# Two expert layers: 240 instead of 256 tokens meet every expert, the others gather their experts' rows

## The chip, the cores and the metric

One core of a Trainium2 chip runs the whole program. The metric is the device time of one execution in microseconds (us). The kernel before took 2565.35 us (median of three runs, 2559.76 to 2567.32). The engines are TensorE (PE; its weight loads are listed apart as PEld), VectorE (DVE), ScalarE (ACT), GpSimd (POOL) and SyncE (SP, which here only queues DMA transfers).

## What is computed

One inference step of a two-layer decoder trunk for 304 tokens: 16 meta tokens, 256 prompt tokens and 32 sample tokens (8 sequences of 4). Layer 0 mixes tokens by gated linear attention and an RG-LRU, layer 1 by RWKV-7. After each mixer comes a PEER expert layer, which is what the change touches. D is 1024, and there are 128 x 128 = 16384 experts of one neuron each:

```python
def block(xb):                                   # tokens x 1024
    q = (xb @ w_q).reshape(..., 8, 256)          # 8 heads, normalised
    s1 = einsum('thd,hkd->thk', q[..., :128], keys[:, 0])
    s2 = einsum('thd,hkd->thk', q[..., 128:], keys[:, 1])
    # top 16 of each, top 16 of their 256 sums: 16 experts a head
    gate = softmax(sc)
    act = gelu(einsum('thkd,td->thk', u_tab[eidx], xb))
    return einsum('thk,thkd->td', gate * act, v_tab[eidx])
```

So each token uses 8 x 16 = 128 rows of `u_tab` and as many of `v_tab`. The layer's result is LN(alpha * x + peer(x)). All is float32. The 16 meta tokens' outputs are dropped at the end, so layer 1 computes its expert layer for 288 tokens only.

## The kernel before

The program runs mixer 0, expert layer 0, mixer 1 and expert layer 1 one after the other. `peer(xh, xl, l)` (L747) is an expert layer. The activations lie transposed (128 features x 304 tokens, 8 blocks `k`), as a pair `xh` + `xl` of float32r tiles whose sum is the float32 value; the rows of the profile print such tiles as f32. A product in this split form (`mm3`, L174) is three matmuls for each block: wh*xh, wh*xl, wl*xh.

Two ways of meeting the experts stand side by side. **Dense tokens** (`d0` to `g0`, L752: 256 of them) meet all 16384 experts in 128 steps `e` of 128 experts. `up` (L991) multiplies 128 experts' rows of u with the dense tokens into `ps_u`; ScalarE applies gelu (L1001) and leaves `act`. `weigh` (L1016) multiplies `act` on VectorE by a dense table of gates (zero where a token didn't choose the expert) and splits it. `down` (L1033) multiplies it with 128 rows of v: two tiles of 128 tokens (stationary), two halves of 512 features, three terms, 12 matmuls into `ps_mm`, summed over 124 steps. The last four steps go through `into` (L1049). For the first 24 steps `up` is a plain float32 matmul, which the program issues as two instructions a block; for the other 104 it is the split form. The weights of a step are loaded whole (`raw`, 512 KB), rounded by ScalarE (`wh`, L170), and the rest is taken by VectorE (`wl`, L171).

**Gathered tokens** (`g0` to the end: `ng` is 48 in layer 0, 32 in layer 1) fetch only their own rows. They come in groups of 16 or 32 tokens (`groups`, L756). In a group of n tokens the 128 partitions hold 128/n of each token's 128 row numbers, in n columns. For each column an indirect DMA, issued by GpSimd (`rows`, L1089), brings 128 rows of 4 KB, two columns to a buffer, three buffers (`ab`). `gup` (L1096) multiplies such a column by the token's activations and sums (one VectorE instruction of 128x1024 and an accumulator read), `gdown` (L1107) adds the row times its coefficient to a sum. Before it, `gprep` (L1058) spreads the row numbers, gates and activations over the partitions with the 0/1 matrix `k_rep`; after it, `gsum` (L1117) folds the partitions back with small matmuls against `k_diag`. Layer 0 has 16 + 32 columns for each table, layer 1 has 32: 160 gathers in all.

The dense gate table is made before the main loop: `ggroup` (L951), once for each 8 tokens (32 times a layer), builds one-hot matrices on VectorE (four products, L959 to L962), multiplies them on TensorE (16 matmuls of 128 columns, `ps_s<-ab`) and ScalarE moves them out (L970); every second one is stored to `G` in DRAM. `gates_load` (L1011) reads 8 steps' gates back, 1 MB at a time (`gb<-G`).

The order is planned by due times (`at`, L769, and L1134 to L1195) in units of about a microsecond of the main loop: the queries, the top-16 search, `ggroup` every `gs` = 2.85 units, then from `tw` on one `up` and one `down` every 2 x 2.56 units, with `up` 36 steps ahead. Gathers are spread evenly from 15 units behind `tw` to 40 before the end (`tg` units apart for two columns: 10.6 in layer 0, 15.9 in layer 1), first all of u, then all of v; the multiplies follow `lag` = 20 units behind their gather. The framework's scheduler may still move an instruction ahead of others on its engine when its inputs are there.

Of the kernel before, what the change touches and what calls it, by code (L numbers as in the profile page):

```python
# [32 lines left out]
GN_EPS = 64e-5  # L33
CHUNKS = [(16 * c, 16) for c in range(17)] + [(TP + 4 * s, 4) for s in range(8)]
TT = [(0, 128), (128, 128), (256, 48)]
XW = 3 + TP + 8 * 7
# [3 lines left out]
def _consts():  # L40
# [20 lines left out]
    for s in range(8):  # L61
# [3 lines left out]
    p, r = np.arange(P)[None], np.arange(P)[:, None]  # L65
    c["k_rep"] = np.stack([r == 16 + p % 32, (r == p % 16), (r == p % 32), r // 32 == p // 32, r // 16 == p // 16],
                          axis=1).astype(np.float32)
# [114 lines left out]
class Prog:  # L182
# [564 lines left out]
    def peer(self, xh, xl, l):  # L747
# [3 lines left out]
        d0 = 0 if l == 0 else NM  # L751
        g0 = d0 + 256  # L752
        ng = T - g0
        tiles = [(d0, P), (d0 + P, P), (g0, ng)]
        groups = ([(0, 16)] if ng == 48 else []) + [(ng - 32, 32)]
        with ExitStack() as es:  # L756
# [6 lines left out]
            gb = lambda shape, dt=F32: self.t(pr, shape, dt, "gb", 4)  # L763
            G = self.t(dp, [16, P, P, 16], F32, "G")
            self.extra(pp, 3, 1)
# [19 lines left out]
            keys = gb([P, 16, P])  # L785
            kr = tl([P, 5, P], "k_rep")
            krep, kblk = kr[:, :3, :], kr[:, 3:, :]

# [9 lines left out]
            def whole32():  # L798
                x32.extend(tl([P, 4, 256], n) for n in ("wh", "wl"))
                self.turn.update(wh=-1, wl=-1)  # L800
                for k in range(KB):
                    nc.vector.tensor_tensor(x32[k // 4][:, k % 4, :], f(xh[:, k, d0:d0 + 256]),
                                            f(xl[:, k, d0:d0 + 256]), op=ALU.add)

# [133 lines left out]
            def turn(i):  # L938
                c = slice(i * P, (i + 1) * P)
                for s in range(2):  # L940
                    pt = self.psum("s")
                    nc.tensor.transpose(pt[:, :P], i12[s][i], self.ident)
                    nc.scalar.activation(iT[s][:, c], pt[:, :P], AF.Copy)
                pt = self.psum("s")
                nc.tensor.transpose(pt[:, :P], gates[i], self.ident)
                nc.scalar.activation(gT[0][:, c], pt[:, :P], AF.Copy, scale=GS)
                nc.vector.scalar_tensor_tensor(gT[1][:, c], pt[:, :P], GS, gT[0][:, c], op0=ALU.mult, op1=ALU.subtract)
# [43 lines left out]
            def up(e):  # L991
                wh, wl = wts.pop(("u", e))
                pu = self.psum("u")[:, :256]
                if wl is None:
                    for k in range(KB):
                        mm(nc, pu, wh[:, k, :], x32[k // 4][:, k % 4, :], k == 0, k == KB - 1)
                else:
                    mm3(nc, pu, lambda k: wh[:, k, :], lambda k: wl[:, k, :],
                        lambda k: xh[:, k, d0:d0 + 256], lambda k: xl[:, k, d0:d0 + 256])
                acts[e] = tl([P, 256], "act", NR)  # L1000
                nc.scalar.activation(acts[e], pu, AF.Gelu_apprx_tanh)  # L1001
# [9 lines left out]
            def gates_load(e):  # L1011
                gr.append(gb([P, 16, 8, 16]))
                nc.sync.dma_start(gr[-1].rearrange("p b i t -> p b (i t)"),
                                  G[:, :, e:e + 8, :].rearrange("b p i t -> p b (i t)"))

            def weigh(e):  # L1016

                if e % 8 == 0:
                    gr[0] = gr.pop(1)
                if e >= P - NL:  # L1020
                    ch, cl = (tl([P, 256], "act", NR, F32R) for _ in range(2))
                elif e % 2:
                    cc = tl([P, 2, 256], "qs", 3, F32R)
                    ch, cl = cc[:, 0, :], cc[:, 1, :]
                else:
                    ch, cl = (tl([P, 256], "sc", 6, F32R) for _ in range(2))
                c = acts.pop(e)
                v16 = lambda ap: ap.rearrange("p (b t) -> p b t", t=16)
                self.mark[True] = nc.vector.tensor_tensor(v16(c), v16(c), gr[0][:, :, e % 8, :], op=ALU.mult)
                split(nc, c, ch, cl)  # L1030
                coef[e] = ch, cl

            def down(e):  # L1033
                if e == 0:
                    Y.extend(self.psum("mm") for _ in range(4))
                args = *wts.pop(("v", e)), *coef.pop(e)
                if e >= P - NL:
                    ends.append(args)
                    return

                vh, vl, ch, cl = args
                for i in range(2):
                    for j, (c, v) in enumerate(((ch, vh), (ch, vl), (cl, vh))):
                        for q in range(2):
                            mm(nc, Y[2 * q + i], c[:, i * P:(i + 1) * P],
                               v[:, 4 * q:4 * q + 4, :].rearrange("p k d -> p (k d)"),
                               e == 0 and j == 0, e == P - NL - 1 and j == 2)
# [10 lines left out]
            def gprep():  # L1058
# [11 lines left out]
                for g, (r0, n) in enumerate(groups):  # L1070
                    er, gt, eg = tl([P, n], f"er{g}", 1, I32), tl([P, n], f"gt{g}"), tl([P, n], "gres", 2)
                    o = 0 if n == 32 else 1
                    rep = krep[:ng, 2 * l + o, :]
                    for src, dst in ((ei, eg), (gates[2], gt)):
# [80 lines left out]
            for i in range(2):  # L1155
                at(tg + 0.1 * i, turn, i)
            for q in range(32):
                at(tg + 1 + pp_["gs"] * q, ggroup, q)
            tw = tg + 1 + 32 * pp_["gs"] + pp_["gl"]

            for j, step in enumerate(pairs(1)):
                at(tg + 1.1 + pp_["gs"] * (8 + 1.5 * j), step)
            at(tg + 1.1 + pp_["gs"] * 31, gprep)
            ahead, u0, u1 = pp_["ahead"], pp_["u0"], pp_["us1"]
# [18 lines left out]
            te = tw + 2 * tu * (P - ahead) + tu * ahead  # L1183
            tg = (te - pp_["te"] - 15 - t1) / (2 * len(gc))
            for j, (g, c) in enumerate(gc):
                for s, fn, tab in ((0, gup, "u"), (len(gc), gdown, "v")):
                    late(t1 + tg * (j + s), rows, tab, g, c)
                    for r in range(2):
                        late(t1 + tg * (j + s + pp_["gj"] * r) + self.lag, fn, g, c, r)
            for g in range(len(groups)):  # L1190
                late(t1 + tg * len(gc) + self.lag - 0.5, gact, g)
            late(te - pp_["te"], gsum)
# [21 lines left out]
            for k in range(KB):  # L1214
                if k % 2 == 0:
                    YT[k // 2] = self.psum("u" if k < 4 else "mm")
                o = YT[k // 2][:, (k % 2) * 256:(k % 2) * 256 + 256]
                for j, args in enumerate(ends):
                    into(o, k, *args, j == 0 and k % 2 == 0, False)
                for i in range(2):  # L1220
                    mm(nc, o[:, i * P:(i + 1) * P], Ys[:, 2 * (k // 4) + i, (k % 4) * P:(k % 4 + 1) * P], self.ident,
                       False, i == 1)
# [587 lines left out]
```

## Time and profile before

| | |
|---|---|
| median of 3 runs | 2565.35 us (2559.76 to 2567.32) |
| the profiled execution | 2568.89 us |
| its span, first to last instruction | 2567.1 us |
| mean granted TensorE clock | 0.965 |
| busy: PE, DVE, ACT, POOL | 94%, 72%, 45%, 21% of the span |
| moved by DMA | 489.73 MB, 191 GB/s over the span |

All times in the profile count from the first instruction. The profiled execution took 1.8 us more than its span. A matmul's busy time contains its way through the array and overlaps the next one's, so the pace of a stream of matmuls is read from their starts, not from their mean length. The stages, by the instructions' times: mixer 0 to about 210 us, the queries and the search to 350, the one-hot products from 352 to 474, the main loop of layer 0 from 493 to 1110; mixer 1 to about 1630; layer 1's one-hot products from 1778 to 1898, its main loop from 1918 to 2527, the end at 2567.

### The profile page before, as it was taken

How to read it: one execution, taken by the hardware profiler on the slowest of the kernel's cores; microseconds unless marked ns; L12 is line 12 of the kernel's file. 1: busy time of each engine (PE TensorE's matmuls, PEld its weight loads, DVE VectorE, ACT ScalarE, POOL GpSimd, SP SyncE). 2: the span in 40 equal slices, each digit the busy share in tenths (PEclk: the TensorE clock that was granted, in tenths of full speed). 3: DMA queues.
4: the chain of work that ended last, by engine and by line, in shares of the span. 5: the costliest groups of instructions: out<-in, count | busy, mean ns of one | idle time of the engine just before them, and what ended most of it. 6: DMA issues, size and time to landing. Idle time of an engine off the chain costs nothing.

```text
span 2567.1 us, 41284 instructions
## 1 busy us (share of the span) xinstructions
PE 2420.2 (94%) x15394; PEld 2073.1 (81%) x15402; DVE 1854.4 (72%) x4200; ACT 1155.6 (45%) x2054; POOL 550.5 (21%) x620
## 2 busy tenths in 40 slices
PE   7989989899999999988999988899989999999997
PEld 5878879799998898865666656787979999989986
DVE  5555898777767888766777785679767766677775
ACT  7524335444444445523544443432444444444453
POOL 3435100011111222024334233520010101121200
PEclk9978999999999999989999999899999999999998
DMA  5323246897879978622111102323679767797662
GB/s 160 114 73 124 99 153 229 283 308 284 285 272 304 364 274 286 240 94 85 48 50 46 40 29 91 119 89 140 233 261 314 245 245 254 261 338 263 242 220 72
DMA packets 197873, 489.73 MB, mean 191 GB/s; under 512 B 21396, under 2 KB 91428, under 8 KB 192936
## 3 DMA queue, kind: packets, MB, share of 16 engines
q1 hardware_dynamic: 173480, 401.10, 44.6%
q0 software_dynamic: 23040, 83.90, 9.7%
q8 instruction: 121, 1.98, 0.3%
q10 hardware_dynamic: 1152, 2.10, 0.2%
q14 instruction: 80, 0.66, 0.1%
HBM read 447.41 MB, written 39.63 MB: 190 GB/s over the span
## 4 chain that ended last, share of the span: by engine, by line
PE 75%; DVE 13%; issue 3%; DMA 3%; ACT 3%; POOL 2%; SPq 1%; POOLq 0%; ACTq 0%; DVEq 0%
PE ps_mm L162 33%; PE ps_u L162 24%; PE ps_s L162 7%; PE ps_pj L162 4%; PE ps_iv L162 3%; DMA gb<-G 3%; PE ps_ch L162 1%; DVE wl L171 1%; PE ps_po L162 1%; DVE ab L921 1%; ACT wh L170 0%; DVE ab L923 0%; DVE x L1575 0%; DVE x L375 0%; DVE ab L918 0%
## 5 line engine op out<-in xcount | busy, mean ns | idle before, releaser
L170 ACT ACTIVATE wh<-raw 128x1024 fp32r<-128x1024 f32 x529 | 560.3, 1060 | 634.4 <-PE ps_u L162 302.1
L171 DVE TENSOR_TENSOR wl<-raw,wh 128x1024 fp32r<-128x1024 f32 x481 | 594.2, 1236 | 301.9 <-ACT wh L170 295.9
L162 PE MATMUL ps_u<-xh,wl 128*128 128x256 f32 x1664 | 469.8, 282 | 5.5 <-DVE wl L171 5.5
L162 PE MATMUL ps_u<-xh,wh 128*128 128x256 f32 x1664 | 471.8, 284 | 2.6 <-ACT act L1001 2.6
L162 PE MATMUL ps_u<-xl,wh 128*128 128x256 f32 x1664 | 468.2, 281 | 0.0
L162 PEld LDWEIGHTS ps_u<-xh,wh 128*128 128x128 f32 x1664 | 314.7, 189 | 11.4 <-ACT act L1001 3.0
L162 PEld LDWEIGHTS ps_u<-xl,wh 128*128 128x128 f32 x1664 | 314.4, 189 | 8.9 <-issue 0.8
L162 PEld LDWEIGHTS ps_u<-xh,wl 128*128 128x128 f32 x1664 | 314.3, 189 | 6.9 <-DVE wl L171 6.6
L162 PE MATMUL ps_mm<-wh,sc 128*128 128x512 f32 x992 | 292.0, 396 | 12.3 <-ACT sc L170 12.3
L162 PE MATMUL ps_mm<-wh,qs 128*128 128x512 f32 x992 | 291.8, 396 | 0.0
L1092 POOL DMA_INDIRECT ab<-in_u,er x80 | 76.8, 961 | 862.9 <-DVE ab L1099 478.7
L162 PEld LDWEIGHTS ps_mm<-wh,sc 128*128 128x128 f32 x992 | 181.8, 190 | 46.6 <-ACT sc L170 12.7
L162 PEld LDWEIGHTS ps_mm<-wh,qs 128*128 128x128 f32 x992 | 181.5, 189 | 35.0
L1092 POOL DMA_INDIRECT ab<-in_v,er x80 | 103.8, 1298 | 431.6 <-DVE gb L1113 339.2
L162 PE MATMUL ps_mm<-wl,sc 128*128 128x512 f32 x496 | 155.4, 395 | 0.1
L162 PE MATMUL ps_mm<-wl,qs 128*128 128x512 f32 x496 | 155.2, 394 | 0.0
L1001 ACT ACTIVATE act<-ps_u 128x256 f32<-128x256 f32 x256 | 94.1, 368 | 105.8 <-PE ps_u L162 105.8
L162 PE MATMUL ps_mm<-xh,wh 128*128 128x304 f32 x416 | 134.0, 326 | 8.1 <-ACT xh L353 4.2
L162 PE MATMUL ps_s<-ab 128*128 128x128 f16 x1024 | 133.6, 296 | 1.7 <-ACT gb L970 1.3
L162 PE MATMUL ps_mm<-xh,wl 128*128 128x304 f32 x416 | 130.1, 313 | 3.9 <-POOL wl L171 3.3
L171 POOL TENSOR_TENSOR wl<-raw,wh 128x1024 fp32r<-128x1024 f32 x48 | 115.2, 2405 | 79.9 <-ACT wh L170 72.5
L162 PE MATMUL ps_mm<-xl,wh 128*128 128x304 f32 x416 | 130.4, 314 | 1.8 <-POOL xl L358 1.8
(559 smaller groups left out, 4492.2 us busy)
## 6 DMA issues: line engine op xcount, KB each, us to landing
raw<-in_ut SPq DMA_DIRECT2D x256, 512.0 KB
raw<-in_v SPq DMA_DIRECT2D x256, 512.0 KB
G<-gb SPq DMA_DIRECT2D x32, 1024.0 KB
gb<-G SPq DMA_DIRECT2D x32, 1024.0 KB
raw<-in_wq SPq DMA_DIRECT2D x32, 512.0 KB
raw<-in_w_in SPq DMA_DIRECT2D x20, 512.0 KB
raw<-in_w_out SPq DMA_DIRECT2D x8, 512.0 KB
raw<-in_w_k SPq DMA_DIRECT2D x8, 512.0 KB
```

Of the source, the lines that this page charges most:

```text
L162: nc.tensor.matmul(out, lhsT, rhs, start=start, stop=stop, skip_group_check=True)
L170: nc.scalar.activation(h, src, AF.Copy)
L171: return (eng or nc.vector).tensor_tensor(l, src, f(h), op=ALU.subtract)
L921: nc.vector.tensor_tensor(eqj, eqj, ib[:n, :, None, :].to_broadcast([n, 16, 16, nh]), op=ALU.mult)
L1001: nc.scalar.activation(acts[e], pu, AF.Gelu_apprx_tanh)
L1092: nc.gpsimd.indirect_dma_start(out=w[:, j, :], out_offset=None, in_=a[f"{tab}{l}"], in_offset=bass.IndirectOffsetOnAxis(ap=gst[g][0][:, c ...
```

## The change

The number of dense tokens becomes a parameter, 240 in both layers. Layer 0 gathers for 64 tokens in two groups of 32, layer 1 for 48 in groups of 16 and 32. So the gathered columns are 64 and 48 for each table, 224 gathers in all. All operands over dense tokens become 240 wide: `up`, the one-hot products (30 for 32 `ggroup`s), the gate table, `weigh`, `into`. `down` keeps two tiles of 128 tokens, the second one from token 112 on; where the results are transposed back, only the last 112 of the second are taken. The constant `k_rep` gets one more matrix. The lag between a gather and its use becomes the least of 20, 2.4 `tg` and 14 + `tg`/2: 18.0 units in layer 0 (where `tg` is now 7.9) and 19.3 in layer 1 (10.6). The diff, cut to its core:

```diff
+ND = (240,240)
...
         d0 = 0 if l == 0 else NM
-        g0 = d0 + 256
+        nd = ND[l]
+        g0 = d0 + nd
         ng = T - g0
-        tiles = [(d0, P), (d0 + P, P), (g0, ng)]
-        groups = ([(0, 16)] if ng == 48 else []) + [(ng - 32, 32)]
+        toff = (0, nd - P)
+        tiles = [(d0 + o, P) for o in toff] + [(g0, ng)]
+        groups = [(0, ng - 32)] * (ng > 32) + [(ng - 32, 32)]
+
+        reps = {(0, 16): 1, (0, 32): 2, (16, 32): 0, (32, 32): 3}
...
-            G = self.t(dp, [16, P, P, 16], F32, "G")
+            G = self.t(dp, [nd // 16, P, P, 16], F32, "G")
...
-                c = slice(i * P, (i + 1) * P)
+                c = slice(toff[i], toff[i] + P)
...
-                pu = self.psum("u")[:, :256]
+                pu = self.psum("u")[:, :nd]
                 if wl is None:
                     for k in range(KB):
-                        mm(nc, pu, wh[:, k, :], x32[k // 4][:, k % 4, :], k == 0, k == KB - 1)
+                        mm(nc, pu, wh[:, k, :], x32[k // 4][:, k % 4, :nd], k == 0, k == KB - 1)
                 else:
                     mm3(nc, pu, lambda k: wh[:, k, :], lambda k: wl[:, k, :],
-                        lambda k: xh[:, k, d0:d0 + 256], lambda k: xl[:, k, d0:d0 + 256])
-                acts[e] = tl([P, 256], "act", NR)
+                        lambda k: xh[:, k, d0:d0 + nd], lambda k: xl[:, k, d0:d0 + nd])
+                acts[e] = tl([P, 256], "act", NR)[:, :nd]
...
-                gr.append(gb([P, 16, 8, 16]))
+                gr.append(gb([P, 16, 8, 16])[:, :nd // 16])
...
-                            mm(nc, Y[2 * q + i], c[:, i * P:(i + 1) * P],
+                            mm(nc, Y[2 * q + i], c[:, toff[i]:toff[i] + P],
...
-            for q in range(32):
+            for q in range(nd // 8):
                 at(tg + 1 + pp_["gs"] * q, ggroup, q)
-            tw = tg + 1 + 32 * pp_["gs"] + pp_["gl"]
+            tw = tg + 1 + (nd // 8) * pp_["gs"] + pp_["gl"]
...
-            at(tg + 1.1 + pp_["gs"] * 31, gprep)
+            at(tg + 1.1 + pp_["gs"] * max(nd // 8 - 1, 27.75), gprep)
...
+            lag = min(self.lag, 2.4 * tg, 14 + tg / 2)
             for j, (g, c) in enumerate(gc):
                 for s, fn, tab in ((0, gup, "u"), (len(gc), gdown, "v")):
                     late(t1 + tg * (j + s), rows, tab, g, c)
                     for r in range(2):
-                        late(t1 + tg * (j + s + pp_["gj"] * r) + self.lag, fn, g, c, r)
+                        late(t1 + tg * (j + s + pp_["gj"] * r) + lag, fn, g, c, r)
...
-                    mm(nc, o[:, i * P:(i + 1) * P], Ys[:, 2 * (k // 4) + i, (k % 4) * P:(k % 4 + 1) * P], self.ident,
+                    mm(nc, o[:, i * P:nd if i else P], Ys[:, 2 * (k // 4) + i, (k % 4) * P:(k % 4 + 1) * P], self.ident[:, i * (2 * P - nd):],
```

## Rows read from the trace of the kernel before

**Rows 1.** The page, part 1: busy time of each engine.

```profile
PE 2420.2 (94%) x15394; PEld 2073.1 (81%) x15402; DVE 1854.4 (72%) x4200; ACT 1155.6 (45%) x2054; POOL 550.5 (21%) x620
```

**Rows 2.** The page, part 4: the chain that ended last, by engine.

```profile
PE 75%; DVE 13%; issue 3%; DMA 3%; ACT 3%; POOL 2%; SPq 1%; POOLq 0%; ACTq 0%; DVEq 0%
```

**Rows 3.** Stretches: length, busy of PE, PEld, DVE, ACT, POOL, clock, DMA share, GB/s.

```profile
362.00:490.00 128.00, 123.76 (x911) 114.12 (x908) 100.17 (x180) 59.16 (x99) 6.15 (x6) 1.00 0.67 243
...
510.00:780.00 270.00, 270.00 (x1736) 245.80 (x1735) 200.06 (x275) 132.55 (x194) 39.45 (x42) 1.00 0.82 288
780.00:1020.00 240.00, 235.95 (x1504) 213.86 (x1503) 192.89 (x240) 115.66 (x171) 60.28 (x50) 1.00 0.89 306
...
1930.00:2230.00 300.00, 300.00 (x1918) 272.33 (x1917) 204.82 (x275) 147.14 (x215) 30.21 (x32) 1.00 0.76 263
2230.00:2440.00 210.00, 208.52 (x1333) 188.72 (x1332) 158.07 (x200) 102.45 (x151) 44.72 (x32) 1.00 0.83 283
```

**Rows 4.** The chain in order of time, main loop of layer 0: start, us, what.

```profile
503.60 2.85 PE ps_u L162 x24
506.45 2.75 PE ps_mm L162 x12
```

**Rows 5.** Timeline of PE, a query projection of layer 0; 12 starts apart.

```profile
222.01 0.30 PE L162 MATMUL ps_mm<-xh,wl 128*128 128x304 f32 x1
...
223.69 0.30 PE L162 MATMUL ps_mm<-xh,wl 128*128 128x304 f32 x1
```

**Rows 6.** Timelines of PE: the sum in layer 1, and two float32r products of mixer 1.

```profile
2512.25 1.87 PE L162 MATMUL ps_s<-k_diag,gb 128*128 128x32 f32 x16
...
1233.64 0.22 PE L162 MATMUL ps_iv<-wh,tx 128*128 128x128 f32 x1
...
486.90 0.28 PE L162 MATMUL ps_u<-xl,wh 128*128 128x256 f32 x1
```

**Rows 7.** The chain in the one-hot stage of layer 0.

```profile
372.20 1.89 PE ps_s L162 x16
374.09 3.46 PE ps_u L162 x16
```

**Rows 8.** Groups of instructions, 362 to 490 us: count, busy and mean, idle before.

```profile
L962 DVE TENSOR_TENSOR ab<-ab,gT 128x1024 f16<-128x1024 f16 x57 | 37.0, 682 | 0.0
...
L162 PE MATMUL ps_u<-wl,raw 128*128 128x256 f32 x62 | 14.7, 379 | 0.0
```

**Rows 9.** The chain at the start of layer 0's main loop.

```profile
478.51 14.38 DMA gb<-G
```

**Rows 10.** Groups on DVE by form, 550 to 800 us, and 780 to 1090 us.

```profile
L171 DVE TENSOR_TENSOR wl<-raw,wh 128x1024 fp32r<-128x1024 f32 x90 | 110.3, 1225 | 59.0 <-ACT wh L170 58.4
L1099 DVE SCALAR_TENSOR_TENSOR ab<-ab,gb 128x1024 f32<-128x1024 f32 x43 | 52.4, 1218 | 0.0
...
L1099 DVE DVE_READ_ACCUMULATOR ab<-ab,gb 128x1 f32 x43 | 3.5, 82 | 0.0
...
L1113 DVE SCALAR_TENSOR_TENSOR gb<-ab,ha,gb 128x1024 f32<-128x1024 f32 x46 | 58.8, 1279 | 0.0
```

**Rows 11.** The page, part 3: the queue that holds the gathers alone.

```profile
q0 software_dynamic: 23040, 83.90, 9.7%
```

**Rows 12.** A stretch of 20 us in layer 0, columns as in rows 3.

```profile
850.00:870.00 20.00, 17.11 (x110) 15.36 (x109) 15.93 (x22) 8.21 (x12) 6.12 (x4) 1.00 1.07 361
```

**Rows 13.** PE's waits, 820 to 860 us, and the one in layer 1's timeline.

```profile
PE ps_u L162 <- DVE wl L171: 4.0, 3, 2.9
...
2277.30 0.39 PE L162 MATMUL ps_u<-xh,wl 128*128 128x256 f32 x1 [1.41 <-DVE wl L171]
```

**Rows 14.** The chain at layer 0's sum of the gathered rows.

```profile
1091.36 4.01 PE ps_s L162 x32
1095.37 16.53 PE ps_mm L162 x60
```

**Rows 15.** The gathers' tile, 550 to 810 us: from issue to landing.

```profile
DMA to landing us min/median/max: 4.2/5.7/7.2
```

More of the change, by code (lines that the diff above doesn't have):

```diff
@@ L65, in _consts @@
     p, r = np.arange(P)[None], np.arange(P)[:, None]
-    c["k_rep"] = np.stack([r == 16 + p % 32, (r == p % 16), (r == p % 32), r // 32 == p // 32, r // 16 == p // 16],
+    c["k_rep"] = np.stack([r == 16 + p % 32, (r == p % 16), (r == p % 32), r == 32 + p % 32,
+                             r // 32 == p // 32, r // 16 == p // 16],
                           axis=1).astype(np.float32)
@@ L785, in peer @@
             keys = gb([P, 16, P])
-            kr = tl([P, 5, P], "k_rep")
-            krep, kblk = kr[:, :3, :], kr[:, 3:, :]
+            kr = tl([P, 6, P], "k_rep")
+            krep, kblk = kr[:, :4, :], kr[:, 4:, :]
             vals2 = tl([P, 16, 2, 16], "vals"), tl([P, 8, 2, 16], "valsg")
@@ L801, in whole32 @@
                 for k in range(KB):
-                    nc.vector.tensor_tensor(x32[k // 4][:, k % 4, :], f(xh[:, k, d0:d0 + 256]),
-                                            f(xl[:, k, d0:d0 + 256]), op=ALU.add)
+                    nc.vector.tensor_tensor(x32[k // 4][:, k % 4, :nd], f(xh[:, k, d0:d0 + nd]),
+                                            f(xl[:, k, d0:d0 + nd]), op=ALU.add)
             qst, pq0 = {}, []
@@ L1020, in weigh @@
                 if e >= P - NL:
-                    ch, cl = (tl([P, 256], "act", NR, F32R) for _ in range(2))
+                    ch, cl = (tl([P, 256], "act", NR, F32R)[:, :nd] for _ in range(2))
                 elif e % 2:
                     cc = tl([P, 2, 256], "qs", 3, F32R)
-                    ch, cl = cc[:, 0, :], cc[:, 1, :]
+                    ch, cl = cc[:, 0, :nd], cc[:, 1, :nd]
                 else:
-                    ch, cl = (tl([P, 256], "sc", 6, F32R) for _ in range(2))
+                    ch, cl = (tl([P, 256], "sc", 6, F32R)[:, :nd] for _ in range(2))
                 c = acts.pop(e)
@@ L1072, in gprep @@
                     o = 0 if n == 32 else 1
-                    rep = krep[:ng, 2 * l + o, :]
+                    rep = krep[:ng, reps[r0, n], :]
                     for src, dst in ((ei, eg), (gates[2], gt)):
@@ L1188, in peer @@
                     for r in range(2):
-                        late(t1 + tg * (j + s + pp_["gj"] * r) + self.lag, fn, g, c, r)
+                        late(t1 + tg * (j + s + pp_["gj"] * r) + lag, fn, g, c, r)
             for g in range(len(groups)):
-                late(t1 + tg * len(gc) + self.lag - 0.5, gact, g)
+                late(t1 + tg * len(gc) + lag - 0.5, gact, g)
             late(te - pp_["te"], gsum)
@@ L1216, in peer @@
                     YT[k // 2] = self.psum("u" if k < 4 else "mm")
-                o = YT[k // 2][:, (k % 2) * 256:(k % 2) * 256 + 256]
+                o = YT[k // 2][:, (k % 2) * 256:(k % 2) * 256 + nd]
                 for j, args in enumerate(ends):
```

## The prediction

> **What bounds the kernel now.** I read the busy shares first [rows 1], then the shares of the chain that ended last [rows 2], then busy time by stage [rows 3], then the chain itself in the stages that the change touches. TensorE is busy 94% of the span and makes 75% of the chain. By stage it is sharper: in the two long expert loops (about 493 to 1110 us, and 1918 to 2527 us) TensorE has no idle time to speak of, while VectorE is busy 74 to 80% in layer 0 and 68 to 75% in layer 1, with the DMA engines at 82 to 89% and 76 to 83% [rows 3]. One expert there is an `up` of 24 matmuls in 2.85 us and a `down` of 12 in 2.75 us, back to back [rows 4]. So TensorE is the bound, and the reader has to ask of each edit whether it shortens a TensorE instruction, or only loads an engine that has room.
>
> **What the change removes.** *Up projections.* 104 experts a layer take the split form, 24 matmuls each, and their moving operand falls from 256 to 240 columns. Now one comes every 2.85/24 = 118.8 ns [rows 4]. Matmuls of the same kind with 304 columns come every (223.69 - 222.01)/12 = 140 ns [rows 5]. The slope is 21.2/48 = 0.44 ns a column, so 16 columns are worth 7.1 ns. That is the upper bound. The lower one comes from what doesn't shrink: every matmul still loads 128 columns of weights. Matmuls of 32 columns behind such loads come every (1.87 - 0.28)/15 = 106 ns (0.28 being one matmul's own length), those of 128 columns in the one-hot products every 1.89/16 = 118 ns [rows 6, 7]. If the second is the floor of any load, only 0.6 ns is gained. I take 6 ns, close to the slope: the f32 weights of the 106 ns row are the same kind as here, while the 118 ns row loads f16 with a stride. Of the 104, 92 lie in the main loop: 92 x 24 x 2 layers x 6 ns = 26.5 us, all on the path.
>
> A page's rule speaks against this. The Trainium skill, "TensorE: Matmul & The Clock Gate", sections "Back-to-back issue gap" and "LDWEIGHTS (loading the stationary operand)", gives N/2.4 + 2.5 ns for a matmul and P/1.2 for a load. By this page of the Trainium skill that is 109 ns at 256 columns and, with the load's 107 ns as the floor, 107 ns at 240: an estimate of 2.5 ns saved on each, 11 us in place of 26.5. The trace doesn't agree on the level, 118.8 ns against 109 at 256 columns; of the floor at 240 no row here shows anything.
>
> *The one-hot stage* (362 to 490 us and its twin): TensorE is busy 123.8 of 128 us [rows 3], so it is nearly as tight. Two of 32 token groups go in each layer, 16 matmuls or 1.89 us each [rows 7]: 2 x 2 x 1.89 = 7.6 us. The plain f32 `up` matmuls, 3.46/16 = 216 ns each [rows 7], stream in proportion to columns, so 16 of 256 are 13.5 ns; about 120 a layer lie here (62 of one of their two halves [rows 8]): 3.2 us. 12 split `up`s a layer: 12 x 24 x 2 x 6 ns = 3.5 us. Sum 14.3 us. On VectorE a token group is 4 products of 0.68 us [rows 8], so 2 groups are 5.5 us a layer, 11 us in all; where the stage is VectorE's turn that is the gain. I take 12 us, bounds 8 to 15. The other 15 plain `up`s lie earlier, beside the top-16 search on VectorE, and give nothing.
>
> *The gate tables.* The first read of the table is on the path, 14.38 us [rows 9], with one sixteenth less to read: 0.9 us a layer. I take 1 us for both, bounds 0 to 2. `down` keeps two tiles of 128 tokens, which now overlap by 16, so its 12 matmuls cost what they did.
>
> **What it adds.** *Gathers.* 16 more row sets for each table and layer: 64 gathers, 64 VectorE multiplies of 1.22 us with an accumulator read of 0.08 or of 1.28 us [rows 10], 64 issues on the POOL queue. The 160 gathers now take 9.7% of 16 engines' span [rows 11], 0.097 x 2567/160 = 1.56 us each, so 32 more are 50 us of transfer a layer. Cover on DMA: between 510 and 1020 us layer 0 has 435 us of transfer; with 46 more it has 481 in a stretch that shrinks to about 497, 97%; layer 1 goes from 402 to 448, 90%. Cover on VectorE: 16 more a phase at 1.3 us are 21 us in each half of the loop, from 74 to about 84% and from 80 to about 90% in layer 0. POOL is 21% busy and only queues gathers there [rows 1]. So the cover holds on average, and is thin in layer 0. Where it is thin now is visible: between 810 and 890 us the gate tables for the second half of the experts come in beside the rows, the DMA share reaches 1.07 [rows 12], where it is 0.82 up to 780 us, and TensorE waits 4.0 us in three pieces for VectorE's split of late weights [rows 13]. Layer 1 gets the row pace that layer 0 has now (48 row sets a table), so I give it 3 us of such waits; layer 0, a third denser, 8 us more than now. The waits of today, 4.0 and 1.4 us [rows 13], could also vanish if the tables fall elsewhere: bounds -1.4 to 6, and -4 to 25 (half of the 50 us uncovered).
>
> *The second gather group of layer 1.* Its rows are summed on TensorE by 16 more matmuls, 4.01 - 1.87 = 2.1 us at most, and in layer 0, where the sum is already of 32 matmuls, the `down`s behind it are slow: 60 in 16.53 us, where 12 take 2.75 [rows 4, 6, 14], 2.8 us lost. 4 us, bounds 1.7 to 4.9. Its preparation (matmuls with the repeat matrix, a few small VectorE operations) comes where TensorE is about to wait 14 us for the gate table anyway [rows 9], so nothing; without that cover about 3 us. The shorter lag between a gather and its use (18 for 20 units, a unit being about 1.1 us) costs nothing while rows land in 7.2 us at the longest [rows 15]; later rows would hold up the weight splits queued behind their multiply on VectorE, and TensorE behind those.
>
> **Sum.** 26.5 + 12 + 1 - 3 - 8 - 4 = 24.5 us. The profiled execution took 2568.9 us, 1.8 outside its span; it lies 3.5 us above the median of the runs shown. 2565.4 - 24.5 = 2541 us. With every bound good: 31.4 + 15 + 2 + 1.4 + 4 - 1.7 = 52 us, 2513 us.
>
> **Rivals.** *The weight load sets the pace.* At 240 columns a pair stays at about 118 ns, as the 128-column one-hot matmuls do [rows 7]. Then the main loop gives 4416 x 0.6 = 2.6 us for 26.5 and the 12 split `up`s 0.3 for 3.5: 2541 + 27 = 2568 us; at half of the gain, 2554 us. The rule of the Trainium skill cited above ("TensorE: Matmul & The Clock Gate") is a mild form of this; by its 2.5 ns each the time would be about 2558 us, an estimate. For the rival: 118 ns at half the columns. Against it: the 106 ns row [rows 6], and the slope between 256 and 304. Chance 0.18.
>
> *VectorE falls behind in layer 0, slower than before.* Between 550 and 800 us VectorE spends 110 us on weight splits, 56 us on row multiplies, and waits 59 us for ScalarE's rounded weights [rows 10]. Some 45 experts pass there, so an expert takes about 3.1 us without rows, with one row set 4.4, with two 5.7, and TensorE's turn falls to about 5.45 us. Now nearly every expert has one row set; after it 128 - 92 = 36 have two. If the 1.3 us wait for ScalarE stays, such an expert takes 7.0 us, 1.55 too many: 36 x 1.55 = 56 us, in place of the 8, 2541 + 48 = 2589 us. It decides from about 0.9 us each (36 x 0.9 = 32 us, the forecast's gain with its 8 us). Against it: the wait for ScalarE is slack that VectorE gives up when it is late, and split weights have buffers ahead; in the burst at 810 us VectorE makes far more than one extra operation an expert and TensorE loses 4 us. Chance 0.15.
>
> *Narrow matmuls lose the fast format.* If under 256 columns this split format fell to the plain f32 rate, 216 against 119 ns [rows 4, 7], the 4992 `up`s would cost over 400 us more. A split-format matmul of 128 columns takes 0.22 us against 0.28 with 256 [rows 6], 0.47 ns a column, so it doesn't at 128. Chance 0.02. That the change doesn't do what it says can't be meant here: the widths are in the code.
>
> **Numbers.** Forecast 0.63, load pace 0.18, VectorE 0.15, format 0.02, others 0.02. A measurement can tell about 0.3%, 7.7 us, from no change. Faster: 0.60 of the forecast and 0.04 of the load pace, 0.64. Same: 0.03 and 0.12, 0.15, and 0.02 of the VectorE rival, 0.17. Slower: the rest, 0.19. The range goes from the good bounds, 2513 us, to 2580 us, which takes in the load's pace and the milder half of the VectorE rival. The forecast's own range is 2513 to 2560 us.
>
> **What would show it.** Right: in the chain of the changed kernel an `up` of 24 in about 2.70 us and `down` still in 2.75; 480 one-hot matmuls a layer; TensorE's waits for split weights some 10 us longer in layer 0. Wrong: `up` still near 2.85 us (load pace), or TensorE idle spread over the loop of layer 0 behind VectorE at over 95%.

## The result, and the profile after

The changed kernel takes 2605.58 us (median of four runs, 2600.95 to 2612.49), the kernel before 2566.34 us (four runs, 2559.76 to 2577.11). The ratio is 1.0153, with a 95% interval of 1.0121 to 1.0186: slower by 1.5%, where the forecast was 2541 us, faster by 1%. It lies 26 us above the end of the range. The profiled execution took 2606.13 us, with a span of 2603.8 us and a mean granted clock of 0.948.

The page of the changed kernel, busy time by engine and the queue of the gathers, against [rows 1, 11] (in the changed kernel the helpers stand 3 lines further down, the expert layer about 7):

```profile
PE 2410.0 (93%) x15362; PEld 2061.2 (79%) x15362; DVE 1904.9 (73%) x4286; ACT 1147.3 (44%) x2049; POOL 699.0 (27%) x684
...
q0 software_dynamic: 32256, 117.45, 12.9%
```

TensorE has less to do than before and the program is longer, so TensorE waits, and its mean granted clock is lower (0.948 against 0.965). Where, is read from the lengths of the stages, which are differences between the starts of their first instructions (us):

| stage | before | after |
|---|---|---|
| mixer 0 | 211.0 | 218.1 |
| layer 0: queries and search | 144.7 | 140.6 |
| layer 0: one-hot products | 116.8 | 113.6 |
| layer 0: end of one-hot to first `down` | 21.3 | **42.6** |
| layer 0: first to last `down` | 617.7 | 615.0 |
| closing of layer 0, mixer 1 | 523.1 | 526.1 |
| layer 1: queries and search | 143.6 | 139.7 |
| layer 1: one-hot products | 118.0 | 113.5 |
| layer 1: end of one-hot to first `down` | 22.0 | **42.8** |
| layer 1: first to last `down` | 609.5 | 612.1 |
| closing of layer 1 | 39.4 | 39.7 |

The two starts of the main loops lose 21 us each, and the loops themselves, where some 13 us each were to be gained, stay as long as they were. The timeline of TensorE in layer 0, its instructions that waited (the bracket: us idle before it, and who released it) and some that didn't:

```profile
484.48 0.28 PE L165 MATMUL ps_u<-xl,wh 128*128 128x240 f32 x1
484.60 0.27 PE L165 MATMUL ps_u<-xh,wl 128*128 128x240 f32 x1
498.59 0.57 PE L165 MATMUL ps_u<-xh,wh 128*128 128x240 f32 x1 [13.72 <-ACT act L1008]
...
499.17 0.41 PE L165 MATMUL ps_u<-xh,wl 128*128 128x240 f32 x1
499.38 0.41 PE L165 MATMUL ps_u<-xh,wh 128*128 128x240 f32 x1
...
510.74 0.57 PE L165 MATMUL ps_u<-xh,wl 128*128 128x240 f32 x1 [6.44 <-DVE wl L174]
...
833.74 1.22 PE L165 MATMUL ps_mm<-wl,qs 128*128 128x512 f32 x2 [5.65 <-DVE wl L174]
...
840.67 0.38 PE L165 MATMUL ps_u<-xh,wl 128*128 128x240 f32 x1 [1.97 <-DVE wl L174]
...
847.81 0.73 PE L165 MATMUL ps_mm<-wl,sc 128*128 128x512 f32 x2 [2.34 <-DVE wl L174]
```

The first wait is for a gelu on ScalarE that frees `ps_u`, the others for weight splits on VectorE. Before, there was one wait of 6 us at this start.

The waits are 14 us of the 21 lost in layer 0, and 2.5 are an `up` that now falls behind the one-hot products instead of between them. The rest is the clock: ahead of the first wait the split matmuls come every 0.12 us, behind it every 0.21 us, since the clock granted had fallen from 2.4 to 1.2 GHz while TensorE stood idle. The stretch around the start, after and before (columns as in [rows 3], the clock third from the right):

```profile
470.00:535.00 65.00, 44.71 (x266) 38.93 (x265) 33.44 (x72) 21.28 (x36) 5.89 (x6) 0.79 0.88 260
```

```profile
470.00:513.00 43.00, 37.08 (x231) 31.66 (x231) 26.37 (x54) 19.61 (x34) 6.15 (x6) 0.92 1.00 326
```

So we ask each queue what stood ahead of that gelu and of those splits. ScalarE after:

```profile
494.39 0.40 ACT L173 ACTIVATE sc<-act 128x240 fp32r<-128x240 f32 x1 [13.69 <-DVE act L1036]
...
497.24 1.04 ACT L173 ACTIVATE wh<-raw 128x1024 fp32r<-128x1024 f32 x1
498.19 0.35 ACT L1008 ACTIVATE act<-ps_u 128x240 f32<-128x240 f32 x1
```

The gelu, whose `ps_u` was ready, stands behind the split of a coefficient, which waits for a weighting on VectorE. VectorE after:

```profile
493.94 1.05 DVE L1036 TENSOR_TENSOR act<-act,gb 128x240 f32<-128x240 f32 x3 [14.87 <-DMA gb<-G]
...
499.05 1.21 DVE L174 TENSOR_TENSOR wl<-raw,wh 128x1024 fp32r<-128x1024 f32 x1
500.18 7.09 DVE L1036 TENSOR_TENSOR act<-act,gb 128x240 f32<-128x240 f32 x22
509.14 0.41 DVE L1036 TENSOR_TENSOR act<-act,gb 128x240 f32<-128x240 f32 x1 [1.87 <-DMA gb<-G]
509.46 1.22 DVE L174 TENSOR_TENSOR wl<-raw,wh 128x1024 fp32r<-128x1024 f32 x1
```

VectorE stands 14.87 us at a weighting whose gate table hasn't landed, and then does 22 weightings in a row, for experts that TensorE needs much later, between one weight split and the next. SP's queue after, the loads it issues:

```profile
480.93 17.95 SPq L1020 DMA_DIRECT2D gb<-G  x4
500.29 0.35 SPq L252 DMA_DIRECT2D raw<-in_v  x1
502.20 6.40 SPq L1020 DMA_DIRECT2D gb<-G  x3
510.71 1.19 SPq L252 DMA_DIRECT2D raw<-in_ut  x1
```

And the same queue in the kernel before:

```profile
478.51 0.38 SPq L1013 DMA_DIRECT2D gb<-G  x1
484.22 0.33 SPq L249 DMA_DIRECT2D raw<-in_ut  x1
484.60 0.43 SPq L1013 DMA_DIRECT2D gb<-G  x1
488.38 5.63 SPq L249 DMA_DIRECT2D raw<-in_v  x1
...
496.56 0.44 SPq L1013 DMA_DIRECT2D gb<-G  x1
```

Before, one table and one or two weight blocks take turns. After, seven tables go with one weight block among them, and from 480.93 to 500.29 no weight load is issued: between 475 and 515 us the tables' loads wait 10.2 us, in four pieces, for VectorE's weightings and 6.9 us for the table's last store to DRAM. The Trainium skill, "Perfetto Trace Analysis", section "DMA Instruction — HWDGE (DVE, Sync)", has the sequencer wait for an instruction's semaphores and come free for the next one only after its descriptors are made; this trace agrees, with 19.4 us in which no load behind goes out. The first table itself is hardly later: VectorE's first weighting starts at 493.94 us here, at 492.92 before. What changed is the order of the queues. All three orders are fixed when the program is built, and no line of the diff names it.

The groups of the weightings, all 256 of the program, before and after (count, busy us, mean ns, idle before them):

```profile
L1029 DVE TENSOR_TENSOR act<-act,gb 128x256 f32<-128x256 f32 x256 | 100.6, 421 | 28.5 <-DMA gb<-G 28.5
```

```profile
L1036 DVE TENSOR_TENSOR act<-act,gb 128x240 f32<-128x240 f32 x256 | 95.5, 405 | 51.9 <-DMA gb<-G 51.9
```

### The profile page after: what moved, and what is told of

It reads as the page before. It is cut to its first block, busy times and chain, and to the rows that moved or that the text cites. A ratio compares the mean times of both kernels' runs of the same rounds, so it can differ in the third digit from the quotient of the medians.

```text
span 2603.8 us, 41450 instructions
## 1 busy us (share of the span) xinstructions
PE 2410.0 (93%) x15362; PEld 2061.2 (79%) x15362; DVE 1904.9 (73%) x4286; ACT 1147.3 (44%) x2049; POOL 699.0 (27%) x684
## 5 line engine op out<-in xcount | busy, mean ns | idle before, releaser
L165 PE MATMUL ps_u<-xh,wh 128*128 128x240 f32 x1664 | 467.3, 281 | 25.2 <-ACT act L1008 25.2
L165 PE MATMUL ps_u<-xh,wl 128*128 128x240 f32 x1664 | 465.8, 280 | 15.7 <-DVE wl L174 15.6
L165 PE MATMUL ps_u<-xl,wh 128*128 128x240 f32 x1664 | 465.1, 280 | 0.0
L1099 POOL DMA_INDIRECT ab<-in_u,er x112 | 151.6, 1354 | 830.4 <-DVE ab L1106 458.6
L165 PEld LDWEIGHTS ps_u<-xh,wh 128*128 128x128 f32 x1664 | 323.1, 194 | 33.7 <-ACT act L1008 25.6
L165 PEld LDWEIGHTS ps_u<-xh,wl 128*128 128x128 f32 x1664 | 323.2, 194 | 17.0 <-DVE wl L174 16.8
L1099 POOL DMA_INDIRECT ab<-in_v,er x112 | 176.5, 1576 | 371.3 <-DVE gb L1120 305.1
L1120 DVE SCALAR_TENSOR_TENSOR gb<-ab,ha,gb 128x1024 f32<-128x1024 f32 x108 | 138.8, 1285 | 0.2
L165 PE MATMUL ps_s<-ab 128*128 128x128 f16 x960 | 124.9, 296 | 12.3 <-DVE ge L914 6.4
L1106 DVE SCALAR_TENSOR_TENSOR ab<-ab,gb 128x1024 f32<-128x1024 f32 x112 | 135.5, 1219 | 0.0
```

The lines of the kernel that those rows point to most:

```text
L165: nc.tensor.matmul(out, lhsT, rhs, start=start, stop=stop, skip_group_check=True)
L1099: nc.gpsimd.indirect_dma_start(out=w[:, j, :], out_offset=None, in_=a[f"{tab}{l}"], in_offset=bass.IndirectOffsetOnAxis(ap=gst[g][0][:, c ...
L1106: nc.vector.scalar_tensor_tensor(w[:, j, :], w[:, j, :], 1.0, xr, op0=ALU.mult, op1=ALU.mult, accum_out=ha[:, c + j:c + j + 1])
L1120: nc.vector.scalar_tensor_tensor(y, w[:, j, :], ha[:, c + j:c + j + 1], y, op0=ALU.mult, op1=ALU.add)
```

## The experiments

**Theory A** is that the order makes the loss, and that the 240-column `up` alone brings the order about. **Theory B** is that the added gathers make it, through the DMA queues and VectorE. Times are medians, ratios are to the kernel before on the same chip.

### One half of the change at a time

`e_gather`, gathers for 64 and 48 tokens, 256 dense:

```diff
-ND = (240,240)
+ND = (256, 256)
+NG = (240, 240)
...
-        g0 = d0 + nd
+        g0 = d0 + NG[l]
...
```

> The gathers of the change alone: 64 and 48 tokens gather rows, as after the change, while all 256 tokens still meet every expert (the 16 tokens that are in both sets are computed twice and their gathered sums are not used). Theory A, the order: the loss comes from the order in which the loads of the gate tables and the weightings are issued, which the 240-column up products alone bring about; the order of this kernel is interleaved as in the kernel before, so it stands within 10 us of it, 2560 to 2578 us. Theory B, the gathers: one more group's or half a group's rows on the DMA queues and more sums on VectorE hold back the weights; then this kernel pays the loss and has not the 27 us that shorter up products give back, 2600 to 2635 us.

Measured: 2576.0 us, ratio 1.0049 (1.0028 to 1.0071). As theory A has it. The gathers cost about 11 us, not 39.

`e_narrow`, 240 dense, the old gathers:

```diff
-        g0 = d0 + nd
+        gz = d0 + nd
+        g0 = d0 + 256
...
+                nc.vector.tensor_scalar(z(k)[:, gz:g0], xk[:, gz:g0], ALPHA, None, op0=ALU.mult)
```

> The 240 columns alone: 240 tokens meet every expert, and gathers stay at 48 and 32 tokens (16 tokens of each layer get no expert's result at all). Theory A: the clumped order of gate tables and weightings is there with the 240 columns, so the loss is there without one added gather: 2592 to 2608 us. Theory B: without the added gathers only the shorter up products and the shorter one-hot stage are left: 2530 to 2545 us.

Measured: 2597.1 us, ratio 1.0134 (1.0088 to 1.0181). Most of the loss without one added gather. Theory B falls.

### Only the width of `up`

`e_up256`, the whole change with `up` over 256 columns:

```diff
...
-                pu = self.psum("u")[:, :nd]
+                pf = self.psum("u")[:, :256]
+                pu = pf[:, :nd]
...
-                        lambda k: xh[:, k, d0:d0 + nd], lambda k: xl[:, k, d0:d0 + nd])
+                        lambda k: xh[:, k, d0:d0 + 256], lambda k: xl[:, k, d0:d0 + 256])
```

> All of the change, but the up products are computed over 256 columns (the last 16 columns are not used), so that each costs 118 ns as before and not 112. Theory A: with 256 columns the order is interleaved again, the starts of the main loops lose their 21 us each, and the time is near the kernel before: 2552 to 2575 us, faster than the changed kernel although its TensorE does 26 us more work. Theory B: the gathers cost what they cost in the changed kernel and the up products 26 us more: 2620 to 2640 us.

Measured: 2576.2 us, ratio 1.0047 (1.0024 to 1.0070), at the upper end of theory A's bounds and 1 us past it. With more TensorE work it beats the changed kernel by 29 us.

`e_up240`, the kernel before with `up` over 240 columns:

```diff
-                pu = self.psum("u")[:, :256]
+                pu = self.psum("u")[:, :240]
...
-                        lambda k: xh[:, k, d0:d0 + 256], lambda k: xl[:, k, d0:d0 + 256])
+                        lambda k: xh[:, k, d0:d0 + 240], lambda k: xl[:, k, d0:d0 + 240])
...
-                nc.scalar.activation(acts[e], pu, AF.Gelu_apprx_tanh)
+                nc.scalar.activation(acts[e][:, :240], pu, AF.Gelu_apprx_tanh)
+                nc.scalar.activation(acts[e][:, 240:], pu[:, 224:], AF.Gelu_apprx_tanh)
```

> The kernel before with nothing changed but the width of the up products: they take the first 240 of the 256 tokens (the last 16 tokens are weighted with other tokens' activations, by a second small gelu in each step). Theory A: that alone clumps the gate tables and the weightings, so the kernel is slower than before although TensorE does 26 us less: 2585 to 2610 us. Rival: another part of the change (16 slabs of the gate tables made 15, the narrower gelu and weightings) brings the loss: 2535 to 2550 us.

Measured: 2588.5 us, ratio 1.0105 (1.0063 to 1.0146). As theory A has it: this one operand's width is enough. (The edit also adds a small gelu in each step; the changed kernel has none and loses, and `e_up256`, which has none either and differs from it in the width of `up` alone, doesn't.) SP's queue at the start of layer 0's main loop in `e_up240`:

```profile
487.91 18.37 SPq L1014 DMA_DIRECT2D gb<-G  x4
507.06 1.59 SPq L249 DMA_DIRECT2D raw<-in_ut  x1
510.41 3.07 SPq L1014 DMA_DIRECT2D gb<-G  x2
```

and in `e_up256`:

```profile
481.21 0.38 SPq L1021 DMA_DIRECT2D gb<-G  x1
487.69 0.33 SPq L252 DMA_DIRECT2D raw<-in_v  x1
488.06 0.62 SPq L1021 DMA_DIRECT2D gb<-G  x1
490.79 9.02 SPq L252 DMA_DIRECT2D raw<-in_ut  x1
```

The narrow `up` clumps the tables in a kernel that is otherwise the old one; the wide `up` keeps them apart in a kernel that is otherwise the new one. The weightings wait 52.1 us in the first and 22.7 us in the second.

### The order written down

`f_pinw` is the changed kernel with two pins. A table's load goes behind the weight load that the program issues last before it, and a weighting behind the weight split that is last before it on VectorE:

```diff
-        nc.sync.dma_start(raw, src)
+        self.lastsp = nc.sync.dma_start(raw, src)
...
+                with self.tc.issue_after(getattr(self.lastsp, "ins", self.lastsp)):
+                    nc.sync.dma_start(gr[-1].rearrange("p b i t -> p b (i t)"),
+                                      G[:, :, e:e + 8, :].rearrange("b p i t -> p b (i t)"))
...
+                with self.tc.issue_after(getattr(self.mark[True], "ins", self.mark[True])):
+                    w_ = nc.vector.tensor_tensor(v16(c), v16(c), gr[0][:, :, e % 8, :], op=ALU.mult)
+                self.mark[True] = w_
```

> The changed kernel with the order written down: each load of a gate table is issued behind the weight load that is last issued before it in the program, and each weighting by the gates behind the weight split that is last before it on VectorE. Theory A: the 40 us at the two loop starts and the waits further on go, and the forecast's gains are left: 2530 to 2560 us. Theory B: the order is no cause, and the time stays at 2595 to 2610 us.

Measured: 2549.4 us, ratio 0.9945 (0.9920 to 0.9970). The instructions are those of the changed kernel, only the queues' order differs, and 56 us are gone. This version beats both kernels.

`b_pinw`, the same two pins in the kernel before:

> The kernel before, with 256 tokens and its own gathers, and the same two pins. If the pins give something of their own, this is faster than before; if the order of the kernel before was already good, it stands within 8 us of it, 2557 to 2573 us, and the 16 us by which the pinned changed kernel beats it are the change's own. Rival: the pins alone give those 16 us and the change gives nothing even in a good order: 2545 to 2553 us.

Measured: 2563.3 us, ratio 1.0007 (0.9982 to 1.0032): the old order was good already, and the gain of `f_pinw` is the change's own.

`n_pinw` is `e_narrow` with the two pins:

> 240 tokens meet every expert, gathers stay at 48 and 32 tokens (16 tokens of each layer get no expert's result), in the pinned order. Its distance to the pinned changed kernel's 2549 us is the price of the added gathers where the order is right. If they are hidden but for the sums of layer 1's second group: 2541 to 2547 us; if they delay weights by DMA and VectorE work: 2530 to 2540 us.

Measured: 2538.1 us, ratio 0.9890 (0.9856 to 0.9924). In a good order the narrow layer gives 2563.3 - 2538.1 = 25 us, and the added gathers take 2549.4 - 2538.1 = 11 us of it back (12.5 if each is set against the kernel before on its own chip). The time is that of the second of the two cases.

### Which of the two queues

`f_pin`, the pin on the tables' loads alone (the first two edits of `f_pinw`):

> The changed kernel with only the loads of the gate tables put back between the weight loads; the weightings on VectorE keep the place that the schedule gives them. Theory A1: the four loads in a row on SP's queue are what holds up the start (the raw weights behind them arrive late); then 40 us go with them, 2545 to 2565 us, close to the 2549 of the kernel with both pinned. Theory A2: the row of 22 weightings ahead of the weight splits on VectorE and the coefficient splits ahead of the gelu on ScalarE cost most of it; then 2575 to 2600 us.

Measured: 2777.9 us, ratio 1.0831 (1.0786 to 1.0876). Both theories missed, by 180 us. The weightings' group and then VectorE's timeline in `f_pin`:

```profile
L1037 DVE TENSOR_TENSOR act<-act,gb 128x240 f32<-128x240 f32 x256 | 91.5, 408 | 243.2 <-DMA gb<-G 243.2
```

```profile
574.44 0.08 DVE L1107 DVE_READ_ACCUMULATOR ab<-ab,gb 128x1 f32 x1
583.94 1.05 DVE L1037 TENSOR_TENSOR act<-act,gb 128x240 f32<-128x240 f32 x3 [9.42 <-DMA gb<-G]
```

The loads are evenly spaced now, one for eight steps, and each comes as late as the program asks. The weightings still stand early in VectorE's queue, in rows of eight, so VectorE reaches the first one of each table before the table: 32 times, up to 15.2 us each. Splits of weights stand behind it. The pin moved VectorE's order too: the changed kernel had 22 weightings in a row at the start and then one or two at a time. So `f_pin` isn't the changed kernel with one queue put right, and what the clumped loads would cost with this order on VectorE no run shows.

Nor is the idle time all of the loss. In the two main loops TensorE stands idle for 152 us, in `f_pinw` for 4, and the loops are 205 us longer: 148 us of waits, and 57 us in which the same instructions take longer, at a mean granted clock of 0.92 and 0.94 against 0.99.

`f_w` pins the weightings alone (the last edit of `f_pinw`):

> The changed kernel with only the weightings pinned, each behind the weight split before it on VectorE; the loads of the gate tables keep the place the schedule gives them (three in a row ahead of the first weight load at each loop start, one by one further on). Theory L, loads in a row on SP's queue hold up the weights behind them whatever VectorE does: 10 us or so of each loop start stay, 2560 to 2585 us. Theory W, what holds TensorE up is VectorE standing at a weighting whose table is late, with weight splits queued behind it, and the loads are harmless: 2545 to 2555 us, as with both pinned.

Measured: 2556.6 us, ratio 0.9961 (0.9937 to 0.9985), between the two forecasts. Against `f_pinw` the median is 7 us longer, or 4 if each is set against the kernel before on its own chip; in the profiles the two main loops are 3.8 and 2.8 us longer. SP's queue in `f_w` still has tables in a row:

```profile
478.07 13.05 SPq L1020 DMA_DIRECT2D gb<-G  x3
491.17 3.26 SPq L252 DMA_DIRECT2D raw<-in_v  x1
```

Yet its loop start takes 23.1 us from the last one-hot product to the first `down`, as in `f_pinw`. The weightings' group in `f_w`:

```profile
L1037 DVE TENSOR_TENSOR act<-act,gb 128x240 f32<-128x240 f32 x256 | 105.5, 412 | 12.8 <-DMA gb<-G 12.8
```

So the weightings' place on VectorE decides: it alone gives 49 of the 56 us. Three loads in a row do no harm at this start; what makes the loops a little longer was not separated. Whether the fourth, and the three after it, do was not separated: with the weightings in turn, the buffers come free in turn and the schedule spreads those loads by itself.

`b_pin`, the loads' pin alone in the kernel before:

> The kernel before, 256 tokens and its own gathers, with only the loads of the gate tables pinned behind the weight loads. If the loss is a matter of order and not of the width of the up products, a kernel of 256 columns must lose too when VectorE comes to a table's first weighting before the table is there: 2620 to 2790 us, with VectorE's idle time at the weightings well over the 28.5 us of before. If narrow up products are needed for the loss, it stays near before, 2557 to 2580 us.

Measured: 2571.7 us, ratio 1.0026 (1.0007 to 1.0045). The loss that I expected didn't come, and the time is that of the other case, in which narrow `up`s are needed for it; yet VectorE stands longer at the weightings, as expected. The group in `b_pin`, and TensorE's waits in its main loop of layer 0 (us in all, times, longest):

```profile
L1030 DVE TENSOR_TENSOR act<-act,gb 128x256 f32<-128x256 f32 x256 | 97.7, 427 | 94.3 <-DMA gb<-G 94.3
```

```profile
PE ps_mm L162 <- DVE wl L171: 0.5, 1, 0.5
```

Against the kernels with both pins, VectorE's 94 us of idle time go with 8 us (2571.7 against 2563.3), its 243 us with 229 (2777.9 against 2549.4). The sum isn't what counts, but each stand less what lies ready for TensorE: in `b_pin` the 32 stands are 2.9 us in the mean and 5.5 at the longest, and the split weights that lie ready outlast nearly all of it. In `f_pin` they are 7.6 us in the mean, and TensorE is idle for most of each (for 8.2 us behind the 9.42 shown above). Its waits over the same stretch are these:

```profile
PE ps_mm L165 <- ACT wh L173: 57.9, 8, 8.9
...
PE ps_mm L165 <- DVE wl L174: 5.7, 9, 1.6
```

The loads' pin without the weightings', then, costs 8 us on the order that the schedule makes with 256 columns and 229 us on the one that it makes with 240. Why VectorE's stands are so much longer with 240 is open. No run has the changed kernel's exact order with 256 columns; that the order and not the width costs the time rests on `f_pinw` and `f_w`, whose `up`s are as narrow.

## Why the prediction was wrong, step by step

**The step that failed** is "The gate tables": it read the first table's 14.38 us [rows 9], took one sixteenth off and gave bounds of 0 to 2 us. The tables had more at stake. Their loads share SP's queue with all weights, and their weightings share VectorE's with all splits, and the prediction took both orders as given, as did its sum. The text ahead of it says that the scheduler may move an instruction ahead of others, and the prediction itself speaks of weight splits queued behind a late multiply; it didn't put the two together. Nor has the sum a term for the clock that falls behind such waits. By stages, the changed kernel against `f_pinw`: the loop starts 42.6 - 23.1 = 19.5 and 42.8 - 21.9 = 20.9 us, the loops 615.0 - 607.7 = 7.3 and 612.1 - 601.4 = 10.7 us, 58 us in all. Why the schedule changes with the width of `up` no run here shows; the runs show that it does.

**The terms of the sum** can be read where the order is good, from `b_pinw` to `n_pinw` for the gains and from `n_pinw` to `f_pinw` for the costs.

*Up projections*: right in size, in part by luck. The chain of `n_pinw` in layer 0's main loop:

```profile
642.02 2.69 PE ps_u L165 x24
644.71 2.78 PE ps_mm L165 x12
```

The median `up` takes 2.694 us for 2.852, so 158/24 = 6.6 ns a matmul where 6 were taken, and 2 x 92 x 0.158 = 29.1 us for 26.5. The load pace of 118 ns, the rival's, is refuted by 112.3, and a lost format falls with it. But a load's floor lies closer than the prediction read. Its 106 ns [rows 6] is the mean of 15 gaps, of which the first is 28 ns, where the row begins behind a `down`; the other 14 are 112 ns each (2512.28 to 2513.84 us), and so are those between the 128x1 matmuls behind such loads (plain float32, both). At 112.3 ns the `up`s have just come down to that. Whether the load holds them there isn't shown, as no run has a narrower one; that nearly all of the 16 columns still paid was luck. The Trainium skill, "TensorE: Matmul & The Clock Gate", section "Back-to-back issue gap", has N/2.4 + 2.5 ns for the gap of a matmul by itself, by which the 16 columns are worth 16/2.4 = 6.7 ns, an estimate that agrees with 6.6; its level, 102.5 ns at 240 columns, is below the measured 112.3.

*`down`*, costed as unchanged, takes 40 ns longer in layer 0 and 30 in layer 1 (medians 2788 for 2748 and 2797 for 2767), spread over its 12 matmuls: 92 x 0.07 = 6.4 us lost. That its second tile now starts at token 112 is one candidate: `e_up256` shares that and has 30 of the 40 and 23 of the 30. The narrow `up` without it, in `e_up240`, has 13 and none. It wasn't tried by itself.

*The one-hot stage*: 12 us taken, 3.2 + 4.1 = 7.3 measured (116.8 to 113.6 and 117.9 to 113.8), and of these some 2.8 us a layer are only moved: one split `up` of nine now falls behind the stage. The products in `b_pinw` and in `n_pinw` (idle before them, and what ended it):

```profile
L162 PE MATMUL ps_s<-ab 128*128 128x128 f16 x1024 | 133.5, 296 | 1.7 <-ACT gb L970 1.3 <-DVE ab L962 0.4
```

```profile
L165 PE MATMUL ps_s<-ab 128*128 128x128 f16 x960 | 125.1, 296 | 12.4 <-DVE ab L970 5.8 <-DVE ge L915 3.2 <-ACT gb L978 3.2
```

960 for 1024, as forecast, but TensorE, with less of its own, now waits 10.7 us more for VectorE and ScalarE, and the mean granted clock of layer 0's stage falls from 1.00 to 0.96: the stage's bound moved. With the wide `up` and as few products, in `e_up256`, the stages take 111.3 us each, 2 us less than with the narrow one. The plain `up`s ahead of it, put at nothing, gave it back: the query stages are 4.4 and 4.2 us shorter, in `e_up240` too and in `e_up256` not. The closing stages, in which the prediction had no term, are 4.5 and 3.9 us longer (the first with mixer 1 in it), with more and longer waits between the last products; this was not taken apart. The two main loops are 17.6 us shorter, where 29.1 - 6.4 would make 22.7; of the 5 us between, 3 are one `up` more in layer 1's loop, and 2 were not traced. The gains were forecast at 26.5 + 12 + 1 = 39.5 us and measured at 25.

*Gathers and sums*: 15 us taken, 11 measured. Layer 0's loop is 607.7 - 601.1 = 6.6 us longer with the added gathers, where 8 were put; layer 1's 3.3 us, all of them behind its last `up`, where the second group's sum had 4 and waits had 3. Two stretches of layer 0's loop in `f_pinw`, columns as in [rows 3]:

```profile
510.00:780.00 270.00, 267.19 (x1737) 238.00 (x1736) 215.40 (x303) 122.13 (x190) 55.15 (x55) 1.00 0.89 313
780.00:1000.00 220.00, 219.44 (x1439) 197.54 (x1438) 185.74 (x224) 104.83 (x163) 57.60 (x53) 1.00 0.94 338
```

VectorE is at 80 and 84%, near the forecast's 84 and 90, and TensorE is idle for 3.4 us of the 490: the cover was thin and held. So the rival that VectorE falls behind fails as well. It had the sign and a time of 2589 us, and in the changed kernel TensorE does wait for weight splits, but not because VectorE has too much to do; it does the wrong thing first. The signs named in the prediction show the limits of such signs: an `up` of 2.70 us and 960 one-hot products are there, and longer waits for split weights too, but with another cause.

All in all, with the order kept, the forecast of 24.5 us becomes 2563.3 - 2549.4 = 14 us against `b_pinw`, and 16 us against the kernel before measured beside it (2565.1).

## What to carry to other kernels

Where a framework's scheduler orders the queues, a change of one operand's size is also a change of order: before adding up what instructions save, ask what the schedule may move, and after a surprise compare the order on every queue before looking at the engines' load. An instruction that waits for a late transfer holds up all that stands behind it on its engine, so what has slack belongs behind what is urgent; write that order down for pairs that meet on one queue, and pin the consumers with the loads, since the loads' pin alone cost 229 us against both here. An engine's idle time is judged piece by piece against the work that lies ready, not by its sum. And behind a long wait, TensorE's slower clock is to be counted as well.

## What the runs showed that I had not expected

The first stage is not as steady as a sum to the microsecond needs. TensorE's instructions come in the same order in `b_pinw` as in the kernel before through mixer 0, yet the stage ended at 217.7 us against 211.0. Two stretches (the clock is the third number from the right), first in the kernel before, then in `b_pinw`:

```profile
120.00:140.00 20.00, 19.91 (x165) 16.93 (x165) 7.63 (x23) 5.08 (x8) 3.46 (x4) 0.79 0.18 61
140.00:160.00 20.00, 18.44 (x88) 10.78 (x89) 9.45 (x22) 5.69 (x14) 6.65 (x8) 0.67 0.13 53
```

```profile
120.00:140.00 20.00, 19.91 (x135) 16.23 (x133) 7.01 (x21) 5.08 (x8) 2.79 (x3) 0.62 0.18 62
140.00:160.00 20.00, 20.00 (x104) 13.70 (x104) 5.11 (x16) 3.40 (x9) 7.92 (x10) 0.53 0.08 33
```

The clock was granted at half (1.2 of 2.4 GHz) for longer in the second, with TensorE as busy up to 120 us in both (19.05 us of the 20 before it). Over the eleven other profiles the stage ended between 214.9 and 220.7 us, so the 7 us that mixer 0 seems to lose in the changed kernel are no part of the change.
